# Attention's masks and first bias tables fetched during the projections, the gates reordered, and two pieces of the third branch done elsewhere

## The chip, the cores and the metric

One core of a Trainium2 chip runs the whole program. The metric is device time in microseconds (us) of one execution; a kernel's time is the median of its runs. A profile of one execution gives the start and length of every instruction on each engine: TensorE (PE, with its weight loads PEld), VectorE (DVE), ScalarE (ACT), GpSimd (POOL), SyncE (SP), and the DMA queues that SP, ACT and POOL issue on.

## The reference

Two layers of an encoder on 512 tokens of width 1024, in float32. Each layer is a half-step SwiGLU, a mixer, and a second half-step SwiGLU, each between RMS norms. The change lies in the mixer:

```python
u = pre(h); one combined projection of u ->
    A: 2-D neighbourhood attention on the 64-wide token grid (rel-pos bias), 8 heads
    B: sliding-window attention, 8 query heads on 2 key/value heads, rotary
    C: differential attention, 4 heads (two softmax maps, learned lambda, rotary)
    per-channel sigmoid gates (one per branch, 1024 channels each)
m = sum_i gate_i * (branch_i @ W_branch_i);  h = h + post(m @ W_out)
```

Branch A adds to its scores a bias table that depends on the head (`rpb`) and a mask for columns outside the window.

## The kernel before

All values are kept with channels on partitions: a 128x512 tile is 128 channels of the 512 tokens. A float32 product is made of three products of high and low parts (fp32r): `mm3` issues lines L326, L327 and L328 for each 128 input channels. Weights are streamed from DRAM as 512 KB tiles `wr` (L211, on SP's queue or ACT's), and split by ACT (L224, high part) and VectorE (L225, low part).

Each layer runs in phases: FFN 1 (`f`), `project` (`p`: most of the projection, by a seven-product scheme in groups; results that the mixer needs in another layout are stored to DRAM as `part` or `raw` by POOL, L1405), `mixer` (`m`: attention, gates, combination, output product), FFN 2 (`f`). Inside `project` and `mixer` a scheduler chooses each engine's order of instructions and the time at which a buffer is taken, from priorities that follow the order in which the code is written. On the chip every engine then works through its own list strictly in order; an instruction that waits holds up all that stands behind it on that engine, DMA issues on SP included.

The mixer's written order is the text `ORDER`, a list of units: `qa`p (load head pair p of branch A: bias tables `braw`, and the halves stacked as `st` tiles from `part`), `aa`p (its attention), `kb`, `qb`p, `ab`p (branch B), `qc`h, `ac`h, `fc`h (branch C: load with rotary, attention, final norm), `ga`/`gb`/`gc`m (gate m of a branch, 24 dense matmuls and a tanh) and `ya`/`yb`/`yc`m (combination m: 12 dense matmuls of the branch's output with `w_branch`, times the gate, added to the sum).

Names and lines that the change touches, in the kernel before:

- `mixer` L1702 to L1712: two tiles `mask` are loaded from `tables` (L1706), `ask` loads `braw` for one head (L1712). `biases` (the adds at L1723) makes a head's `bedge` and `bmid` from `braw` and `mask`, on VectorE. L1662 adds the bias to the scores and takes the row maximum (`nmx`).
- Loads: `load` (L1739), rotary `rope` (L1747 to L1750; VectorE's first operation on the loaded tile is L1748), `restacked` (L1762, L1763: the `st` tiles).
- Gates (L1898, ACT). Those of branch A stay in SBUF in two tiles of the pool `n`, [128, 4, 512] each; the others go to DRAM (L1901) and come back through `load` at their combination.
- `combine`: L1911 (VectorE) multiplies; for branches B and C, L1915 (POOL) adds to `merged[m]`. After that `M` splits `merged` (ACT L355, VectorE L356).
- Branch C's outputs `oc` are split (L352, L353) into tiles of pool `g`, which has 10 buffers; branch A's outputs `oa` are two tiles of pool `X` (6 buffers, four of which hold the operand until the last gate). The output norm's gains (`gain`, four loads on SP, L465) take a tile of pool `X`.
- The buffer that a loaded gate of branch B takes (pool `gd`, 2 buffers) is the one that a fresh gate takes on its way to DRAM.

Of the kernel before, what the change touches and what calls it, by code (L numbers as in the profile page):

```python
# [10 lines left out]
F32 = mybir.dt.float32  # L11
F32R = mybir.dt.float32r
AF = mybir.ActivationFunctionType
ALU = mybir.AluOpType
AX = mybir.AxisListType

P = 128
# [3 lines left out]
T = 512  # L21
# [18 lines left out]
QA, KA, VA, QB, KB, VB, QC, KC, VC, GL = 0, 4, 8, 12, 16, 17, 18, 22, 26, 30  # L40
COVER = (QA, KA, VA, QA + 1, KA + 1, VA + 1, KB, VB)
GROUPS = (
    (QA + 2, KA + 2), (VA + 2, VA + 3), (QA + 3, KA + 3), (QB, QB + 1), (QB + 2, QB + 3), (QC, KC), (QC + 1, KC + 1),
    (VC, VC + 1), (QC + 2, KC + 2), (QC + 3, KC + 3), (VC + 2, VC + 3),
) + tuple((GL + 2 * i, GL + 2 * i + 1) for i in range(0))
# [21 lines left out]
RPBW = 64  # L67
# [2 lines left out]


ORDER = """
qa0 qa1 aa0 ga0 ga1 qa2 aa1 ga2 qa3 aa2 ga3 ga4 kb qb0 aa3 ga5 qb1 ab0
ga6 ga7 gb0 qb2 ab1 gb1 gb2 qb3 ab2 ya0 gb3 ya1 gb4 qc0 ab3 ya2 gb5 ya3
qc1 ac0 gb6 ya4 gb7 qc2 fc0 ac1 ya5 gc0 ya6 fc1 qc3 ac2 gc1 ya7 gc2 fc2
ac3 yb0 gc3 yb1 gc4 fc3 yb2 gc5 yb3 gc6 yb4 gc7 yb5 yb6 yb7 yc0 yc1 yc2
yc3 yc4 yc5 yc6 yc7
"""


# [39 lines left out]
def encoder_kernel(ctx: ExitStack, tc: tile.TileContext, order, xT, wts, cols, rows, rpb, consts, tables, out):  # L120
    nc = tc.nc
# [3 lines left out]
    sb = ctx.enter_context(tc.tile_pool(name="sb", bufs=1))  # L125
# [4 lines left out]
    BUFS = {"X": 6, "n": 2, "wr": 3, "wp": 2, "wq": 2}  # L130
# [16 lines left out]
    def nm(s):  # L147
        serial[0] += 1
        return f"{s}{serial[0]}"

    def big(tag, dt=F32, shape=(P, T), name="v"):
        if tag in BUFS:
            return sb.tile(list(shape), dt, tag=tag, name=nm(name), bufs=BUFS[tag])
        kind, pool = phase[0]
        return pool.tile(list(shape), dt, tag=tag, name=nm(name), bufs=ABUFS[kind][tag])
# [7 lines left out]
    V, A, G, PE = nc.vector, nc.scalar, nc.gpsimd, nc.tensor  # L163

    def f(t):
        return t.bitcast(F32)
# [15 lines left out]
    def col(name, l, b=0, t=None):  # L182
        c = COLS[name, l] + b
        return (colt if t is None else t)[:, c : c + 1]
# [76 lines left out]
    for l in range(L):  # L261
        for which in (1, 2):
            name = f"ffn{which}_w_down"
# [81 lines left out]
    def dense1(name, l, c, X, r0=0, tag="mm", midway=None):  # L345
        return dense([(name, l, r0, c)], X, (tag,), midway=midway)[0]

    def split(src, tag="a", scale=None, shape=(P, T)):
        hi = big(tag, F32R, shape, name="hi")
        lo = big(tag, F32R, shape, name="lo")  # L350
        if scale is None:
            A.activation(hi, src, AF.Copy)  # L352
            V.tensor_tensor(out=lo, in0=src, in1=f(hi), op=ALU.subtract)  # L353
        else:
            A.activation(hi, src, AF.Copy, scale=scale)  # L355
            V.scalar_tensor_tensor(out=lo, in0=src, scalar=scale, in1=f(hi), op0=ALU.mult, op1=ALU.subtract)  # L356
        return hi, lo
# [1010 lines left out]
    def project(l, op, accs):  # L1368
        w, X = "w_in", op.blocks
# [76 lines left out]
        def work(n):  # L1446
            for _ in range(min(n, len(slowly))):
                slowly.pop(0)()
# [32 lines left out]
        made = {}  # L1481
# [38 lines left out]
        for n, c0 in (("cosR", 0), ("sinR", 512)):  # L1520
            t = big("rr", name=n)
# [22 lines left out]

        made["gates"] = []

        def gate_tile(c):
            if (c - GL) % 4 == 0:
                made["gates"].append(sb.tile([P, 4, T], F32, tag="n", name=nm("gate"), bufs=BUFS["n"]))
            return made["gates"][-1][:, (c - GL) % 4, :]  # L1550
# [5 lines left out]
        def second_half(g):  # L1556
            evict(groups[g]["t"], GROUPS[g][0], groups[g]["a"], 1)
            if GROUPS[g][0] < GL:
                ready(GROUPS[g][0], groups[g]["t"])

        def other(g):
            c, v = GROUPS[g][1], groups[g]["v"]
            if c >= GL:
                evict(gate_tile(c), c, v, None, -1.0)
                return
            x = v if form_of(c) == "-" else big("t", name="x")
            evict(x, c, v, None, -1.0)
            ready(c, x)

        for g in range(count):  # L1570
            more, last = g + 1 < count, g + 1 == count
            S.p1(g)
            if g:
                S.add22(g - 1)
            S.low24(g)
            if more:
                S.high1(g + 1)
            S.seed(g)
            if more:
# [12 lines left out]
            if more:  # L1592
                S.high12(g + 1)
            if g:
                other(g - 1)
            S.p6(g)
            if more:
                S.low13(g + 1)
            else:
                ensure(stream["made"] + 2)  # L1600
            S.copy2(g)
            S.p4(g)
            S.add21(g)
            if last:
                S.p5(g)
                S.add22(g)
            S.p2(g)
            first_half(g)
            if more:
                S.low12(g + 1)  # L1610
                S.sum4(g + 1)
                if g + 2 < count:
                    S.fetches(g + 2)
                else:
                    fetch(1, nc.sync)
                S.p5(g)
                S.high24(g + 1)
            work(3)
        S.p3(count - 1)
        second_half(count - 1)  # L1620
        other(count - 1)
        work(len(slowly))
        return made

    def stacks(x, both):
        hi, lo = split(x, "tx")
# [74 lines left out]
    def mixer(l, op, made):  # L1701
        w, X = "w_in", op.blocks  # L1702
        masks, raws, turning = {}, {}, []
        for c0, n in ((0, 512), (512, 256)):
            m = big("g", name="mask")
            nc.sync.dma_start(m[:, :n], tables[:, 1024 + c0 : 1024 + c0 + n])  # L1706
            for b in range(0, n, 256):
                masks[(c0 + b) // 256] = m[:, b : b + 256]

        def ask(hd):  # L1710
            raw = raws[hd] = big("g", name="braw")
            nc.sync.dma_start(raw, bass.AP(rpb.tensor, (l * 8 + hd) * 16 * RPBW, [[RPBW, 8], [1, 16], [1, 8 * RPBW]]))  # L1712

        def biases(hd):
            raw = raws.pop(hd)
# [59 lines left out]
        OT = {}  # L1775
# [51 lines left out]

            pending.append(done)

        oc, totc = [], []  # L1830

        def attn_c(sq, sk, v):
            vh, vl = v
# [50 lines left out]
            follow(rest)  # L1884

        gate, merged = {}, [None] * KD
        gate0 = made["gates"]
        while len(gate0) < 2:
            gate0.append(sb.tile([P, 4, T], F32, tag="n", name=nm("gate"), bufs=BUFS["n"]))
        for _, c in GROUPS:  # L1890
            for m in (c - 1 - GL, c - GL) if c > GL else ():
                gate[0, m] = gate0[m // 4][:, m % 4, :]

        def gates(n, *ms):
            for m in ms:
                pg = dense1(w, l, GL + n * KD + m, X)
                t = gate0[m // 4][:, m % 4, :] if n == 0 else big("gd", name="gate")
                A.activation(t, pg, AF.Tanh, scale=0.5, bias=col("b_gate", l, n * KD + m))  # L1898
                if n:
                    d = dr.tile([P, T], F32, tag="gate", name=nm("gate"), bufs=4 * KD)  # L1900
                    nc.sync.dma_start(d, t)  # L1901
                    t = d
                gate[n, m] = t

        def combine(n, key, *ms):
            for m in ms:
                py = dense1("w_branch", l, m, [OT[key, k] for k in range(4)], r0=n * 4)
                t = gate.pop((n, m))
                if n:
                    t = load(t, tag="gd" if n == 1 else "tx")  # L1910
                V.scalar_tensor_tensor(out=t, in0=t, scalar=1.0, in1=py, op0=ALU.add, op1=ALU.mult)  # L1911
                if n == 0:
                    merged[m] = t
                else:
                    G.tensor_tensor(out=merged[m], in0=merged[m], in1=t, op=ALU.add)  # L1915

        def qkv_b(c):
            return restacked(c, c == KB)
# [10 lines left out]
        def finish_c(hd):  # L1929
            A.activation(totc[hd], totc[hd], AF.Sqrt)  # L1930
            V.reciprocal(out=totc[hd], in_=totc[hd])
            rep = spread(totc[hd], NT)
            V.scalar_tensor_tensor(
                out=oc[hd], in0=oc[hd], scalar=gsub[:, l : l + 1], in1=rep, op0=ALU.mult, op1=ALU.mult
            )
            OT["c", hd] = split(oc[hd], "g")

        held = {}

# [103 lines left out]
    X = accs = None  # L2043
    for l in range(L):
        with open_phase("f"):
            X, accs = ffn(l, 1, X, accs)
        with open_phase("p"):
            made = project(l, X, accs)
        with open_phase("m"):
            X, accs = mixer(l, X, made)  # L2050
        with open_phase("f"):
            X, accs = ffn(l, 2, X, accs)
# [59 lines left out]
```

## Time and profile before

| | us |
|---|---|
| median of 3 runs | 2403.28 (2402.62 to 2405.92) |
| the profiled execution's own time | 2402.72 |
| its span | 2401.0 |
| mixer of layer 0, first to last score and combination | about 507 to 870 |
| mixer of layer 1 | about 1697 to 2058 |

The span is the time from the first instruction to the last. "Busy" on PE means that matmuls are in flight. A row of a timeline gives start, length, engine, line, operation and tiles, and in brackets the idle time in front of it and what ended that; a letter q behind an engine (SPq) is its instruction queue, where DMAs are issued. A list of waits gives, for each pair of waiting line and releaser, the us in total, the times and the longest.

### The profile page before, as it was taken

Reading aid. Unit: us, or ns where it says so; the run is one execution under the profiler, and the core shown is the slowest. Engines: PE = TensorE matmul, PEld = TensorE weight load, DVE = VectorE, ACT = ScalarE, POOL = GpSimd, SP = SyncE. Lnnn points to the kernel's source line nnn. Section 1 sums busy time; section 2 is a strip of 40 time slices with the busy share of each in tenths; the row PEclk is TensorE's granted clock in tenths of the full one; section 3 lists DMA queues with packets and bytes.
Section 4 is the critical chain, followed back from the end, with each engine's and each line's share of the span. In section 5 each row is a group of like instructions: output and inputs, shape, how many; then the busy total and the mean of one; then the engine's idle time right before and its main releaser. Section 6 shows DMA issues by size and latency. Waiting matters only on the chain. (4 is left out here: it accounts for less than half of the span.)

```text
span 2401.0 us, 39975 instructions
## 1 busy us (share of the span) xinstructions
PE 2350.9 (98%) x15062; PEld 2104.9 (88%) x15062; DVE 1874.5 (78%) x3040; ACT 1447.4 (60%) x2711; POOL 205.8 (9%) x258
## 2 busy tenths in 40 slices
PE   9999999999999999999999999999899999999998
PEld 8999889987877789998899998899788777899987
DVE  8887978957977567888878878888488765788796
ACT  6565666658766465555655555666586664656563
POOL 0111001110001300110001110011000012011100
PEclk9999999999999999999999999999999999999999
DMA  5566536667565434655435565366765664346642
GB/s 169 159 174 186 166 131 189 202 199 203 151 191 180 142 118 141 159 167 166 168 97 163 163 176 193 107 206 206 207 188 149 205 189 136 97 148 169 191 145 85
DMA packets 143265, 395.14 MB, mean 165 GB/s; under 512 B 19296, under 2 KB 26080, under 8 KB 142560
## 3 DMA queue, kind: packets, MB, share of 16 engines
q1 hardware_dynamic: 114672, 279.25, 37.5%
q0 software_dynamic: 12992, 57.68, 9.3%
q10 hardware_dynamic: 15408, 55.66, 7.7%
q8 instruction: 118, 1.93, 0.3%
q14 instruction: 75, 0.61, 0.1%
HBM read 326.98 MB, written 80.74 MB: 170 GB/s over the span
## 5 line engine op out<-in xcount | busy, mean ns | idle before, releaser
L680 PE MATMUL mm<-X,h 128*128 128x256 f32 x1472 | 261.5, 277 | 0.0
L225 DVE TENSOR_TENSOR w<-wr,w 128x512 fp32r<-128x512 f32 x272 | 189.2, 706 | 71.0 <-ACT w L224 70.2
L326 PE MATMUL mm<-X,w 128*128 128x512 f32 (+1 forms) x602 | 229.6, 381 | 3.0 <-ACT X L553 1.8
L327 PE MATMUL mm<-X,w 128*128 128x512 f32 (+1 forms) x602 | 229.9, 382 | 0.8 <-DVE X L554 0.7
L328 PE MATMUL mm<-X,w 128*128 128x512 f32 (+1 forms) x602 | 228.3, 379 | 1.7 <-DVE w L225 1.7
L224 ACT ACTIVATE w<-wr 128x512 fp32r<-128x512 f32 x272 | 167.5, 627 | 99.3 <-PE mm L328 54.2
L680 PEld LDWEIGHTS mm<-X,h 128*128 128x128 f32 x1472 | 223.5, 188 | 0.8 <-DVE v L738 0.2
L680 PE MATMUL mm<-ht,l 128*128 128x256 f32 x736 | 205.9, 280 | 0.0
L680 PE MATMUL mm<-ht,h 128*128 128x256 f32 x736 | 205.5, 279 | 0.0
L680 PE MATMUL mm<-lt,h 128*128 128x256 f32 x736 | 204.9, 278 | 0.0
L680 PE MATMUL mx<-ht,h 128*128 128x256 f32 x736 | 203.6, 277 | 0.1
L680 PE MATMUL mx<-lt,h 128*128 128x256 f32 x736 | 203.6, 277 | 0.0
L680 PE MATMUL mm<-X,l 128*128 128x256 f32 x736 | 203.5, 277 | 0.0
L680 PE MATMUL mx<-ht,l 128*128 128x256 f32 x736 | 203.5, 276 | 0.0
L630 DVE TENSOR_TENSOR l<-wr,h 128x1024 fp32r<-128x1024 f32 x92 | 112.5, 1223 | 61.0 <-PE mm L680 60.9
L662 ACT ACTIVATE h<-wr 128x1024 fp32r<-128x1024 f32 x92 | 97.7, 1062 | 72.4 <-PE mx L680 52.7
L680 PE MATMUL at<-X,w 128*128 128x256 f32 x1104 | 141.2, 277 | 0.0
L680 PEld LDWEIGHTS mm<-ht,l 128*128 128x128 f32 x736 | 138.7, 188 | 0.1
L680 PEld LDWEIGHTS mm<-lt,h 128*128 128x128 f32 x736 | 138.7, 188 | 0.0
L680 PEld LDWEIGHTS mm<-ht,h 128*128 128x128 f32 x736 | 138.6, 188 | 0.0
L680 PEld LDWEIGHTS mx<-ht,h 128*128 128x128 f32 x736 | 138.2, 188 | 0.3 <-ACT v L724 0.3
L680 PEld LDWEIGHTS mx<-lt,h 128*128 128x128 f32 x736 | 138.3, 188 | 0.0
(438 smaller groups left out, 6770.7 us busy)
## 6 DMA issues: line engine op xcount, KB each, us to landing
wr<-in_wts_dram SPq DMA_DIRECT2D x269, 512.0 KB
wr<-in_wts_dram ACTq DMA_DIRECT2D x106, 512.0 KB
sum<-in_wts_dram POOLq DMA_DIRECT2D x64, 512.0 KB, 5.0
st<-part SPq DMA_DIRECT2D x120, 128.0 KB
ap<-in_wts_dram SPq DMA_DIRECT2D x20, 512.0 KB
a<-kept SPq DMA_DIRECT2D x32, 256.0 KB
ap<-sum SPq DMA_DIRECT2D x16, 512.0 KB
x<-part SPq DMA_DIRECT2D x32, 256.0 KB
```

The costliest lines, as they stand in the source:

```text
L224: A.activation(hi, raw, AF.Copy)
L225: V.tensor_tensor(out=lo, in0=raw, in1=f(hi), op=ALU.subtract)
L326: PE.matmul(acc, w[0], x[0], start=start, stop=False)
L327: PE.matmul(acc, w[0], x[1], start=False, stop=False)
L328: PE.matmul(acc, w[1], x[0], start=False, stop=stop)
L630: V.tensor_tensor(out=w["l1"], in0=self.raws[g][0], in1=f(w["h1"]), op=ALU.subtract)
L662: A.activation(self.W[g]["h24"], self.raws[g][1], AF.Copy)
L680: PE.matmul(acc, ws[i], xs[j], start=start and k == m == 0, stop=stop and k == n - 1 and m == 2, skip_group_check=True,)
```

## The change

Four things are changed together.

1. `project` gets `tables_of_a`, called in the written order at group 6 of its loop. It takes one tile `pre` of pool `n` and loads both masks and the bias tables of heads 0 and 1 into it; `mixer` uses these parts where it used `mask` and the first two `braw`. The second of branch A's gate tiles can only be taken when `pre` has been read for the last time.
2. `ORDER`: gates gb0 to gb7 stand ahead of ga4 to ga7, and the combinations of branch A come later. All combinations of branch A still precede those of B and C.
3. Branch C's heads 1 to 3 are split into two tiles of pool `X` (`pairs`) instead of tiles of pool `g`. Head 0 stays in `g`.
4. The sum of branch C's part is made on VectorE instead of POOL; branch B's stays on POOL.

```diff
@@ -70,11 +70,11 @@
 ORDER = """
-qa0 qa1 aa0 ga0 ga1 qa2 aa1 ga2 qa3 aa2 ga3 ga4 kb qb0 aa3 ga5 qb1 ab0
...
+qa0 qa1 aa0 ga0 ga1 qa2 aa1 ga2 qa3 aa2 ga3 gb0 kb qb0 aa3 gb1 qb1 ab0
...
@@ -1544,6 +1544,14 @@
+        def tables_of_a():
+            t = sb.tile([P, 4, T], F32, tag="n", name=nm("pre"), bufs=BUFS["n"])
+            nc.sync.dma_start(t[:, 0, :], tables[:, 1024 : 1024 + 512])
+            nc.sync.dma_start(t[:, 1, :256], tables[:, 1024 + 512 : 1024 + 768])
+            for hd in range(2):
+                nc.sync.dma_start(t[:, 2 + hd, :], raw_of(l, hd))
+            made["tables"] = t
+
@@ -1616,11 +1624,16 @@
             work(3)
+            if g == 6:
+                tables_of_a()
...
+    def raw_of(l, hd):
+        return bass.AP(rpb.tensor, (l * 8 + hd) * 16 * RPBW, [[RPBW, 8], [1, 16], [1, 8 * RPBW]])
@@ -1701,15 +1714,16 @@
-        for c0, n in ((0, 512), (512, 256)):
-            m = big("g", name="mask")
-            nc.sync.dma_start(m[:, :n], tables[:, 1024 + c0 : 1024 + c0 + n])
-            for b in range(0, n, 256):
-                masks[(c0 + b) // 256] = m[:, b : b + 256]
+        pre = made["tables"]
+        for n in range(3):
+            masks[n] = pre[:, n // 2, 256 * (n % 2) : 256 * (n % 2) + 256]
 
         def ask(hd):
+            if hd < 2:
+                raws[hd] = pre[:, 2 + hd, :]
+                return
             raw = raws[hd] = big("g", name="braw")
...
@@ -1884,16 +1898,13 @@
-        gate0 = made["gates"]
-        while len(gate0) < 2:
-            gate0.append(sb.tile([P, 4, T], F32, tag="n", name=nm("gate"), bufs=BUFS["n"]))
...
+        gate0 = []
 
         def gates(n, *ms):
             for m in ms:
                 pg = dense1(w, l, GL + n * KD + m, X)
+                if n == 0 and m % 4 == 0:
+                    gate0.append(sb.tile([P, 4, T], F32, tag="n", name=nm("gate"), bufs=BUFS["n"]))
@@ -1912,7 +1923,7 @@
-                    G.tensor_tensor(out=merged[m], in0=merged[m], in1=t, op=ALU.add)
+                    (G if n == 1 else V).tensor_tensor(out=merged[m], in0=merged[m], in1=t, op=ALU.add)
@@ -1933,7 +1944,14 @@
-            OT["c", hd] = split(oc[hd], "g")
+            if hd == 0:
+                OT["c", hd] = split(oc[hd], "g")
+                return
+            if not pairs:
+                pairs.extend(sb.tile([P, 4, T], F32R, tag="X", name=nm("oc"), bufs=BUFS["X"]) for _ in range(2))
+            hi, lo = OT["c", hd] = tuple(t[:, hd, :] for t in pairs)
+            A.activation(hi, oc[hd], AF.Copy)
+            V.tensor_tensor(out=lo, in0=oc[hd], in1=f(hi), op=ALU.subtract)
```

The new `ORDER` as a whole:

```
qa0 qa1 aa0 ga0 ga1 qa2 aa1 ga2 qa3 aa2 ga3 gb0 kb qb0 aa3 gb1 qb1 ab0
gb2 gb3 qb2 ab1 gb4 gb5 gb6 qb3 ab2 gb7 ga4 qc0 ab3 ga5 ga6 qc1 ac0
ga7 ya0 gc0 ya1 qc2 fc0 ac1 gc1 ya2 gc2 ya3 gc3 fc1 qc3 ac2 ya4 ya5
ya6 ya7 yb0 gc4 fc2 ac3 yb1 gc5 yb2 gc6 fc3 yb3 gc7 yb4 yb5 yb6 yb7
yc0 yc1 yc2 yc3 yc4 yc5 yc6 yc7
```

In the changed kernel the lines below the new function are 11 to 14 higher: the bias adds of L1723 stand at L1737, L1662 at L1675, the `st` loads at L1776 and L1777, `braw` at L1726, L1739 at L1753, L1911 at L1922 and L1915 at L1926.

The rows that follow are the order of instructions on one engine (line, operation, written tile and read tiles with buffer numbers), as the two programs have it in layer 0. First SyncE, where the mixer starts; before:

```order
L1706 DMA mask_5789<-in_tables_dram 128x512
L1706 DMA mask_5791<-in_tables_dram 128x256
L1712 DMA braw_5797<-in_rpb_dram 128x1x512
L1712 DMA braw_5799<-in_rpb_dram 128x1x512
L1712 DMA braw_5801<-in_rpb_dram 128x1x512
L1712 DMA braw_5803<-in_rpb_dram 128x1x512
L1762 DMA st_5805<-part_4051 64x512
L1763 DMA st_5805<-part_4053 64x512
```

And with the change, at the same place:

```order
L1726 DMA braw_5796<-in_rpb_dram 128x1x512
L1726 DMA braw_5798<-in_rpb_dram 128x1x512
L1776 DMA st_5800<-part_4051 64x512
L1777 DMA st_5800<-part_4053 64x512
L1776 DMA st_5803<-part_4051 64x512
```

Masks and the tables of the first two heads are gone from here (the two `braw` left are the second pair's). The second `braw` waits for the project's last stores, as a mask did before. The four loads that left stand here on SyncE now, in the middle of the project:

```order
L1549 DMA pre_5225<-in_tables_dram 128x512
L1550 DMA pre_5225<-in_tables_dram 128x256
L1552 DMA pre_5225<-in_rpb_dram 128x1x512 x2
L211 DMA wr_4271<-in_wts_dram 128x1024
L1454 DMA sh_4202<-x_4200 32x512 x4
```

`wr_4271` is the weight tile that was issued at 386.06 us in the profile of before; the four loads were moved to just ahead of it.

Second, VectorE where the mixer starts, around the first bias; before, with the splits of three weight tiles ahead of it:

```order
L1411 TENSOR_TENSOR lo_5777<-at_5771,hi_5776 128x512
L225 TENSOR_TENSOR w_5973<-wr_5971,w_5973 128x512
L225 TENSOR_TENSOR w_5988<-wr_5971,w_5988 128x512
L225 TENSOR_TENSOR w_6184<-wr_6182,w_6184 128x512
L1723 TENSOR_TENSOR bedge_5828<-braw_5797,mask_5789 128x256
L1723 TENSOR_TENSOR bmid_5829<-braw_5797,mask_5789 128x256
```

With the change:

```order
L1411 TENSOR_TENSOR lo_5782<-at_5776,hi_5781 128x512
L225 TENSOR_TENSOR w_5969<-wr_5967,w_5969 128x512
L1737 TENSOR_TENSOR bedge_5823<-pre_5225 128x256
L1737 TENSOR_TENSOR bmid_5824<-pre_5225 128x256
L1737 TENSOR_TENSOR bedge_5823<-pre_5225 128x128 x2
```

Two splits now come after the first bias. Its wait is no longer for `braw` but for the last two `part` stores of POOL's queue.

Third, the tail. SyncE, with the change (gates of branch B, written `x_9038` and so on, are loaded for yb4 to yb7):

```order
L460 DMA h_9305<-kept_3724 128x512 x2
L460 DMA h_9305<-kept_3805 128x512 x2
L465 DMA gain_9314<-in_rows_dram 128x512 x4
L1753 DMA x_9038<-gate_7096 128x512
L1912 DMA gate_9018<-gate_9016 128x512
L1753 DMA x_9058<-gate_7133 128x512
L1753 DMA x_9080<-gate_7170 128x512
L1753 DMA x_9100<-gate_7366 128x512
```

The gains stood some 35 rows earlier before, around a rotary load of branch C: their tile now takes a buffer of the operand, which the gate gc7 reads last. VectorE in the last combinations (yc2 and yc3), with the change:

```order
L1922 SCALAR_TENSOR_TENSOR x_9164<-x_9164,mm_9146 128x512
L225 TENSOR_TENSOR w_9191<-wr_9189,w_9191 128x512
L1926 TENSOR_TENSOR gate_5964<-gate_5964,x_9164 128x512
L1922 SCALAR_TENSOR_TENSOR x_9184<-x_9184,mm_9168 128x512
L356 SCALAR_TENSOR_TENSOR lo_9281<-gate_5964,hi_9280 128x512
L1926 TENSOR_TENSOR gate_5964<-gate_5964,x_9184 128x512
L225 TENSOR_TENSOR w_9211<-wr_9189,w_9211 128x512
```

The two L1926 of these rows were POOL's before, as L1915.

More of the change, by code (lines that the diff above doesn't have):

```diff
@@ L72 @@
 ORDER = """
-qa0 qa1 aa0 ga0 ga1 qa2 aa1 ga2 qa3 aa2 ga3 ga4 kb qb0 aa3 ga5 qb1 ab0
[L74 to L77, printed above, removed]
+qa0 qa1 aa0 ga0 ga1 qa2 aa1 ga2 qa3 aa2 ga3 gb0 kb qb0 aa3 gb1 qb1 ab0
[3 more added lines that the diff above has]
+yc0 yc1 yc2 yc3 yc4 yc5 yc6 yc7
 """
@@ L1703, in mixer @@
         masks, raws, turning = {}, {}, []
-        for c0, n in ((0, 512), (512, 256)):
-            m = big("g", name="mask")
-            nc.sync.dma_start(m[:, :n], tables[:, 1024 + c0 : 1024 + c0 + n])
-            for b in range(0, n, 256):
-                masks[(c0 + b) // 256] = m[:, b : b + 256]
+        pre = made["tables"]
+        for n in range(3):
+            masks[n] = pre[:, n // 2, 256 * (n % 2) : 256 * (n % 2) + 256]
         def ask(hd):
+            if hd < 2:
+                raws[hd] = pre[:, 2 + hd, :]
+                return
             raw = raws[hd] = big("g", name="braw")
-            nc.sync.dma_start(raw, bass.AP(rpb.tensor, (l * 8 + hd) * 16 * RPBW, [[RPBW, 8], [1, 16], [1, 8 * RPBW]]))
+            nc.sync.dma_start(raw, raw_of(l, hd))
         def biases(hd):
@@ L1828, in attn_b @@
             pending.append(done)
-        oc, totc = [], []
+        oc, totc, pairs = [], [], []
         def attn_c(sq, sk, v):
@@ L1886, in mixer @@
         gate, merged = {}, [None] * KD
-        gate0 = made["gates"]
-        while len(gate0) < 2:
-            gate0.append(sb.tile([P, 4, T], F32, tag="n", name=nm("gate"), bufs=BUFS["n"]))
-        for _, c in GROUPS:
-            for m in (c - 1 - GL, c - GL) if c > GL else ():
-                gate[0, m] = gate0[m // 4][:, m % 4, :]
+        gate0 = []
         def gates(n, *ms):
```

## The prediction

> **What bounds the kernel.** I read the page's first part first, then TensorE's waits stage by stage, then the stretches in which those waits fall.
>
> ```profile
> span 2401.0 us, 39975 instructions
> PE 2350.9 (98%) x15062; PEld 2104.9 (88%) x15062; DVE 1874.5 (78%) x3040; ACT 1447.4 (60%) x2711; POOL 205.8 (9%) x258
> ```
>
> TensorE (PE) is busy for all but 50.1 us, and the change leaves its matmuls as they are: what it can win is a part of these 50 us. They are shared out by the four lists below, of TensorE's waits in both layers' mixers: 505 to 560 us (start, layer 0), 560 to 880 (the rest of it), 1695 to 1740 (start, layer 1) and 1740 to 2062 (the rest). Columns: waiting line, releaser, us in total, times, longest.
>
> ```profile
> PE mx L1659 <- DVE nmx L1662: 4.5, 2, 2.3
> PE mx L1659 <- DVE l L1676: 3.0, 1, 3.0
> ...
> PE mm L326 <- DVE x L1911: 3.9, 5, 1.3
> PE o L1870 <- DVE lo L353: 2.0, 1, 2.0
> PE o L1694 <- DVE lo L353: 1.1, 1, 1.1
> ...
> PE mx L1659 <- DMA st<-part: 6.0, 2, 3.5
> PE mx L1659 <- DVE nmx L1662: 2.1, 2, 1.7
> ...
> PE mm L326 <- DVE x L1911: 4.5, 5, 1.7
> PE o L1870 <- DVE lo L353: 1.5, 1, 1.5
> PE o L1694 <- DVE lo L353: 1.5, 1, 1.5
> ```
>
> Three groups: the **start** of branch A (7.5 + 8.1 = 15.6 us), the **middle** (2.0 + 1.1 + 1.5 + 1.5 = 6.1), and the gate combination L1911, nearly all of it at the **tail** (3.9 + 4.5 = 8.4). Together 30.1 us, 1.25% of the span: the most that any rearrangement of the mixer could give back.
>
> **Start: masks and first biases.** Layer 0, in order of time (start, length, engine, line):
>
> ```profile
> 509.76 0.54 POOL L1405 DMA_DIRECT2D part<-lo  x1
> ...
> 514.31 0.33 SPq L1706 DMA_DIRECT2D mask<-in_tables_dram  x1
> 514.83 2.90 SPq L1712 DMA_DIRECT2D braw<-in_rpb_dram  x4
> 517.82 0.53 SPq L1762 DMA_DIRECT2D st<-part  x1
> ...
> 520.08 0.43 DVE L1723 TENSOR_TENSOR bedge<-braw,mask 128x256 f32<-128x256 f32 x1 [2.75 <-DMA braw<-in_rpb_dram]
> ...
> 524.46 0.42 DVE L1723 TENSOR_TENSOR bedge<-braw,mask 128x256 f32<-128x256 f32 x1 [2.54 <-DMA braw<-in_rpb_dram]
> ...
> 507.58 0.40 PE L326 MATMUL mm<-X,w 128*128 128x512 f32 x1
> ...
> 518.49 0.39 PE L326 MATMUL mm<-X,w 128*128 128x512 f32 x1
> ...
> 521.64 0.51 PE L1659 MATMUL mx<-early 128*128 128x256 f32 x2 [2.31 <-DVE nmx L1662]
> ```
>
> SyncE's queue issues in order. The mask waits there for the project's last stores to land, so the four bias loads go out from 514.83 and the first can be added only at 520.08; the score that needs it runs 1.56 us later, at 521.64. The second head pays the same again at 524.46.
>
> With the change both heads' tables are in SBUF long before. The order on VectorE shows that the first L1737 waits instead for the project's last two stores. Their landing:
>
> ```profile
> part<-hi POOLq DMA_DIRECT2D x2, 256.0 KB, 5.0
> part<-lo POOLq DMA_DIRECT2D x2, 256.0 KB, 4.9
> ```
>
> The last is issued at 509.76 and lands 4.9 to 5.0 us on, at 514.7. The put starts there, and with the same 1.56 us TensorE can go on at about 516.3. The program now has 38 dense matmuls instead of 51 ahead of that score; the first and the 49th of them above are 10.91 us apart, 0.227 a matmul, so that 38 last from 507.58 to 516.2. The wait of 2.31 becomes about 0.2, and the second head's goes entirely: nmx in both layers falls from 4.5 + 2.1 to 0.4. Bounds: 0, and the whole 6.6 if the stores land as much later as the loads did.
>
> The other 9.0 us of the start are stacked operands (`st`). SyncE's own waits, layer 0, then layer 1:
>
> ```profile
> SPq L1763 <- DMA wr<-in_wts_dram: 6.0, 1, 6.0
> ...
> SPq L1763 <- DMA wr<-in_wts_dram: 8.0, 2, 4.8
> ```
>
> The 3.0 that the list puts on `l` in layer 0 is the second operand half, held up by the `wr` in the first row: `l` was long done. In the new order two bias loads instead of two masks and four bias loads stand ahead of the `st` loads, which begin about 515.4 instead of 517.82; and the second head pair's `st` no longer wait behind a weight load of ACT's queue. Against that, TensorE asks for its first `st` 12 dense matmuls (2.7 us) and 4.3 us of removed waits sooner. I keep 1.0 us in layer 0 and 2.5 in layer 1 (the size of the wait in layer 1 that no `wr` explains), 3.5 of the 9.0; bounds 0 and 9.0. The start's sum: 15.6 − 0.4 − 3.5 = **11.7 us saved**.
>
> **The fetch itself.** Masks and two heads are 0.9 MB a layer, on SyncE's queue just ahead of the weights that are issued at 386.06. The stretch has:
>
> ```profile
> 380.00:390.00 10.00, 10.00 (x48) 8.26 (x47) 6.81 (x10) 5.85 (x11) 2.16 (x4) 1.00 0.78 247
> ...
> 386.06 0.33 SPq L211 DMA_DIRECT2D wr<-in_wts_dram  x1
> ...
> 393.86 1.04 ACT L625 ACTIVATE h<-wr 128x1024 fp32r<-128x1024 f32 x1
> ```
>
> (The row gives us, PE, PEld, DVE, ACT, POOL busy with counts, clock, DMA share, GB/s.) At 247 GB/s the extra bytes are 3.6 us of transfer; the weights of 386.06 are read 7.8 us later with no wait, and PE is busy for all 10 us. I take 0.5 us a layer, bounds 0 and 3.6.
>
> The Trainium skill, "DMA: Bandwidth & Descriptors", section "Issuing engines are not separate DMA queues", speaks against any such move: transfers from the SyncE, ScalarE and GpSimd queues run on the same 16 engines and interleave, so an early fetch is paid for by whatever else is moving. By it the project's weights and stores would slow by the whole transfer, and the sum would be 6.2 us worse; the trace agrees that a busy stretch stretches transfers, but shows no wait of PE there.
>
> **Tail.** Third part's sums, layer 1:
>
> ```profile
> 2001.00 1.61 POOL L1915 TENSOR_TENSOR gate<-gate,x 128x512 f32<-128x512 f32 x1 [2.13 <-DVE x L1911]
> 2004.74 1.61 POOL L1915 TENSOR_TENSOR gate<-gate,x 128x512 f32<-128x512 f32 x1 [2.13 <-DVE x L1911]
> ...
> 2002.64 0.63 ACT L355 ACTIVATE hi<-gate 128x512 fp32r<-128x512 f32 x1 [2.59 <-POOL gate L1915]
> ...
> 2003.30 0.69 DVE L356 SCALAR_TENSOR_TENSOR lo<-gate,hi 128x512 fp32r<-128x512 f32 x1 [1.85 <-ACT hi L355]
> 2003.91 0.68 DVE L1911 SCALAR_TENSOR_TENSOR x<-x,mm 128x512 f32<-128x512 f32 x1
> ```
>
> It is a loop: add on POOL, high part on ACT, low part L356, then the next L1911 behind it on VectorE, which frees the PSUM bank PE waits for, then POOL again: 3.74 us a turn. PE's 12 matmuls a unit take 12 x 0.227 = 2.73 us, so it waits. On VectorE the add costs what L1911 costs, 0.68: the turn is 3.74 − 1.61 + 0.68 = 2.8, and in half of the pairs L1922 stands ahead of the low part. These waits go. The 8 adds a layer are 5.4 us of VectorE, paid out of its idle 1.85 us a turn.
>
> What stays is the second part's loads:
>
> ```profile
> 1980.31 1.68 POOL L1915 TENSOR_TENSOR gate<-gate,x 128x512 f32<-128x512 f32 x1 [7.41 <-DVE x L1911]
> ...
> 1982.01 12.99 SPq L1739 DMA_DIRECT2D x<-gate  x4
> ...
> 1985.75 0.69 DVE L1911 SCALAR_TENSOR_TENSOR x<-x,mm 128x512 f32<-128x512 f32 x1 [1.72 <-DMA x<-gate]
> ...
> 1986.59 0.47 PE L326 MATMUL mm<-hi,w 128*128 128x512 f32 x1 [1.65 <-DVE x L1911]
> ...
> 1924.21 0.50 PE L326 MATMUL mm<-hi,w 128*128 128x512 f32 x1 [0.95 <-DVE x L1911]
> ```
>
> A load waits for the POOL sum that frees its buffer and takes 1985.75 − 1982.01 = 3.74 us. The new order runs yb4 to yb7 without a gate between them. With 2.73 a unit on PE and 3.74 + 0.69 + 1.68 for a buffer, counted by hand from the end of yb3 (yb4 done at 5.45 + 2.73 = 8.2 with gc7 between): yb5's load is issued at 8.2 + 0.69 + 1.68 = 10.5 and used at 14.2, where PE wanted its bank at 13.7 (about 1.2 wait with L1922 itself); yb7's costs another 0.5 at yc1. So 1.7 us a layer, and the 0.95 of the last row, which lies before the tail, stays. 8.4 becomes 4.4: **4.0 saved**. Bounds: 8.4 saved, or the rival on the slower side below.
>
> The post-norm gains, which used to be loaded early, now wait for gc7 on SyncE and stand ahead of yb4's load:
>
> ```profile
> L465 SPq DMA_DIRECT2D gain<-in_rows_dram x8: 333/422/900, 712.2 to 1904.8; - x8
> ```
>
> Four issues of 0.42 after the middle of gc7 put yb4's load 4.4 us after yb3, landed at 8.1, needed at 8.2: just covered by gc7 and yb4 on PE.
>
> **Middle.** These waits come from VectorE standing in L1748 (branch C's rotary multiply) for its load, with the low part that PE needs behind it; the row, from the list of that line, gives the idle time in us and the times. The change does not touch that; between the first and last attention of branch C ORDER now has 8 gates and 9 combinations where it had 6 and 6, so more cover. I take 0; bounds: all 6.1 gone, or 7.9 lost (all 14.0 us that L1748 waits reaching PE).
>
> ```profile
>   DMA x<-raw: 14.0, 7
> ```
>
> **Sum**, against the profiled execution's own 2402.72 us (0.56 below the median of the runs, 2403.28): 2402.72 − 11.7 − 4.0 + 1.0 = **2388.0 us**.
>
> **Rivals.** (1) *The stores replace the loads.* VectorE, now holding the first put in order, waits for the stores, and `st` stays as late as now: the two second-head waits (4.5 − 2.3 and 2.1 − 1.7, from the nmx rows, so 2.6) and the tail remain as gains: 2402.72 − 2.6 − 4.0 + 1.0 = 2397.1. For it: every `st` still stands behind a store-bound load on SyncE. Against: that load is one, not six. (2) *The fetch is paid in the project*: the weights of 386.06 come later by its whole transfer and PE stands for it, 3.6 instead of 0.5 a layer, so 2388.0 + 6.2 = 2394.2. Against: no wait there now. (It is the case that the section of the Trainium skill named above would have one expect.) (3) *Slower: the tail becomes bound by its loads.* Each us by which yb5's and yb7's loads exceed 3.74 comes back about twice, since they follow one another through the same two buffers. The gains are broadcast loads in one burst with `h` right ahead of them, and a burst of bias loads took 520.08 − 514.83 = 5.3 and more, up to 9 for the second. At 9.5 us a load, a layer's tail costs 1.7 + 2 x 5.8 = 13.3 and the time is 2402.72 − 11.7 − 7.4 + 1.0 + 2 x 13.3 = 2411.2; it is slower than before from some 7.4 us a load. Against: the loads of the rows above took half of that. (4) *The change does not do what it says*: the fetch stays late because its tile is not free early. The order puts it directly ahead of the weights of 386.06 with nothing left to wait for, so this is unlikely: 2402.72 − 4.0 = 2398.7, the tail alone.
>
> **Chances.** Forecast 0.62 (own range 2381 to 2396); stores 0.18; fetch 0.07; slower tail 0.08; not as said 0.05. Range 2380 to 2402: it leaves out the slow tail and a middle that vanishes too. A run here can tell about 0.2%, 4.8 us: faster 0.78 (the forecast, the fetch, half of the stores' case), same 0.13, slower 0.09.
>
> **What would show it.** Right: L1737's first row at about 515, nmx waits under 1 us, the gate L1922 waits after yc1 gone, turns of 2.7 us on VectorE, the rope idle as now. Wrong: SyncE's first `st` after 517; weights waiting around 380 to 400; x<-gate over 5 us at the tail, with L1922 idle for DMA; or new waits of low parts L353 behind a put.

## The result and the profile after

| | before | after |
|---|---|---|
| median of 4 runs, us | 2403.45 (2402.62 to 2405.92) | 2382.69 (2380.20 to 2386.78) |
| the profiled execution's own time | 2402.72 | 2380.20 |
| its span | 2401.0 | 2378.4 |

The ratio of the times is 0.9914 (95%: 0.9896 to 0.9931): the kernel became 20.8 us faster; 15.3 had been forecast. The two profiled executions are 22.5 us apart, and the readings below explain that difference.

First the page of the changed kernel, its busy times:

```profile
PE 2346.9 (99%) x15062; PEld 2105.4 (89%) x15062; DVE 1883.2 (79%) x3056; ACT 1448.5 (61%) x2711; POOL 178.8 (8%) x242
```

TensorE's idle time went from 50.1 to 31.5 us (span less busy), which is 18.6 of the 22.6 us of span. Its *busy* time fell too, by 4.0 us, with the same 15062 matmuls: keep that in mind for the end of this section.

TensorE's waits in the changed kernel's mixers, in four lists as before: start and rest of layer 0, start and rest of layer 1 (505 to 560 us, 560 to 880, 1680 to 1725, 1725 to 2050):

```profile
PE at L1703 <- ACT s L1692: 1.5, 1, 1.5
...
PE mm L326 <- DVE x L1922: 2.2, 1, 2.2
PE o L1707 <- DVE lo L353: 1.9, 2, 1.5
...
PE at L1880 <- DVE s L1871: 0.7, 1, 0.7
...
PE o L1706 <- ACT hi L352: 0.3, 1, 0.3
...
PE at L1703 <- ACT s L1692: 1.3, 1, 1.3
...
PE mm L326 <- DVE x L1922: 2.7, 2, 2.3
PE at L1880 <- DVE s L1871: 1.3, 1, 1.3
PE o L1707 <- DVE lo L353: 1.2, 3, 0.7
...
PE mx L1672 <- DMA st<-part: 0.7, 1, 0.7
...
PE o L1706 <- ACT hi L352: 0.3, 1, 0.3
```

Start: 1.5 + 1.3 + 0.7 = 3.5 us, where it was 15.6. Combination: 2.2 + 2.7 = 4.9, where it was 8.4. The rest: 5.7, where the four lists of before add up to 8.7 once their start, L1911 and the final norm's unchanged waits (L553, L554) are taken out. Together 14.1 against 32.7.

The start of layer 0 in the changed kernel, in order of time:

```profile
514.31 0.66 SPq L1726 DMA_DIRECT2D braw<-in_rpb_dram  x1
...
514.90 0.43 DVE L1737 TENSOR_TENSOR bedge<-pre 128x256 f32<-128x256 f32 x1 [2.35 <-DMA part<-lo]
515.07 0.51 SPq L1776 DMA_DIRECT2D st<-part  x1
```

The first bias is added at 514.90 instead of 520.08, and what releases it is the project's last store (`part<-lo`), not a bias load. The first `st` load goes out at 515.07 instead of 517.82.

What busy time gained is seen in the windows. Columns: stretch, its length, busy time and count of PE, PEld, DVE, ACT, POOL, then the granted clock of TensorE, DMA share and GB/s. Before:

```profile
505.00:560.00 55.00, 47.30 (x242) 39.35 (x242) 27.18 (x90) 33.35 (x88) 2.14 (x4) 0.91 0.71 188
...
524.11:530.94 6.83, 5.65 (x18) 4.77 (x19) 4.16 (x18) 4.90 (x16) 0.00 (x0) 0.50 0.67 182
548.00:551.42 3.42, 2.89 (x9) 2.43 (x10) 0.05 (x1) 0.00 (x0) 0.00 (x0) 0.50 0.68 197
722.08:725.49 3.41, 3.41 (x11) 2.85 (x11) 3.10 (x6) 1.23 (x2) 0.00 (x0) 0.50 0.47 154
1735.84:1739.25 3.41, 2.80 (x9) 2.34 (x10) 0.00 (x0) 0.00 (x0) 0.00 (x0) 0.50 0.78 232
```

After:

```profile
505.00:560.00 55.00, 53.39 (x301) 44.79 (x301) 37.88 (x127) 42.92 (x119) 2.14 (x4) 1.00 0.79 218
...
784.86:788.27 3.41, 3.19 (x8) 2.55 (x9) 1.59 (x3) 0.00 (x0) 2.96 (x2) 0.50 0.48 154
1962.46:1965.87 3.41, 3.28 (x8) 2.63 (x9) 1.29 (x2) 0.00 (x0) 2.94 (x2) 0.50 0.45 156
```

Compare the first rows: the same 55 us hold 301 matmul records instead of 242, but only 6 us more of busy time. Before, matmuls there ran at a mean clock of 0.91. The other rows are all the stretches of the two kernels' mixers in which the granted clock was 0.50. Half of the busy time in them is given away: (5.65 + 2.89 + 3.41 + 2.80) x 0.5 = 7.4 us before, (3.19 + 3.28) x 0.5 = 3.2 after. So by this estimate some 4.1 us of the gain are not waits at all, but the slow matmuls that followed them. The prediction has no such term.

### The profile page after: what moved, and what is told of

Same layout as the page of the kernel before. It is cut to its first block, busy times and chain, and to the rows that moved or that the text cites. A ratio compares the mean times of both kernels' runs of the same rounds, so it can differ in the third digit from the quotient of the medians.

```text
span 2378.4 us, 39981 instructions
## 1 busy us (share of the span) xinstructions
PE 2346.9 (99%) x15062; PEld 2105.4 (89%) x15062; DVE 1883.2 (79%) x3056; ACT 1448.5 (61%) x2711; POOL 178.8 (8%) x242
## 5 line engine op out<-in xcount | busy, mean ns | idle before, releaser
L326 PE MATMUL mm<-X,w 128*128 128x512 f32 (+1 forms) x602 | 228.5, 380 | 2.0 <-ACT X L553 1.8
```

The costliest lines, as they stand in the source:

```text
L326: PE.matmul(acc, w[0], x[0], start=start, stop=False)
```

## The experiments

Times are medians; each kernel is set against runs of the kernel before on the same chip. "The fetch" is part 1 of the change, "the order" part 2, "the pairs" part 3, "the sum" part 4.

| kernel | us | before, us | difference | ratio (95%) |
|---|---|---|---|---|
| sum alone | 2399.67 | 2404.04 | −4.4 | 0.9985 (0.9976 to 0.9993) |
| fetch alone | 2394.84 | 2403.65 | −8.8 | 0.9965 (0.9953 to 0.9977) |
| fetch + sum | 2390.99 | 2402.58 | −11.6 | 0.9951 (0.9940 to 0.9963) |
| fetch + order | 2386.25 | 2402.58 | −16.3 | 0.9928 (0.9915 to 0.9941) |
| fetch + order + sum (no pairs) | 2381.05 | 2404.04 | −23.0 | 0.9907 (0.9894 to 0.9921) |
| whole change | 2382.69 | 2403.45 | −20.8 | 0.9914 (0.9896 to 0.9931) |
| fetch + order + pairs (no sum) | 2391.39 | 2404.04 | −12.7 | 0.9948 (0.9936 to 0.9961) |
| order + pairs + sum (no fetch) | 2405.94 | 2404.04 | +1.9 | 1.0009 (0.9999 to 1.0020) |
| whole change, late gate loads elsewhere | 2376.14 | 2403.65 | −27.5 | 0.9883 (0.9864 to 0.9901) |
| the same without the pairs | 2373.94 | 2403.65 | −29.7 | 0.9876 (0.9862 to 0.9891) |

### The sum alone

```diff
-                    G.tensor_tensor(out=merged[m], in0=merged[m], in1=t, op=ALU.add)
+                    (G if n == 1 else V).tensor_tensor(out=merged[m], in0=merged[m], in1=t, op=ALU.add)
```

> The kernel before with one thing changed: branch C's sum on VectorE. If the loop POOL, ACT, VectorE is what held yc2 to yc7 (the prediction), the L1911 waits of 0.7 us or so at the tail (three in each layer) go and the time falls by 4 to 5 us, to about 2399. If those waits only stand in for the loads of the gates, it stays at 2403.

Measured 4.4 us faster. The list of TensorE's waits has `PE mm L326 <- DVE x L1911: 5.6, 4, 1.9`, where before had 8.4 us in 10 waits: six short waits are gone and four stay. Ahead of two of them, 1.9 us each, VectorE waits for a gate's load; the other two (0.6 and 1.2) lie before the tail.

### The sum back on POOL

The line above undone in the changed kernel.

> The changed kernel with branch C's sum back on POOL. By the loop: waits of about 0.7 us come back at each yc from yc2 on, 4 to 6 us in both layers, so about 2387. If the order or the gates' loads set the tail: no change, 2383.

Measured 8.7 us slower than the changed kernel, more than expected. Ten waits on L1922 are 10.2 us, among them the six that the sum alone had removed: 5.3 more than in the changed kernel, of the 12.0 us between the two profiled executions (2392.18 and 2380.20). Waits for `st` loads and low parts of attention are longer in it as well. The sum is worth 4.4 alone, 2.8 on top of the fetch (11.6 − 8.8), and 6.7 on top of fetch and order (23.0 − 16.3). By the intervals of the table each such difference of two rows is uncertain by some 4 us, so these three can't be told apart.

### Everything but the fetch

```diff
-            if g == 6:
-                tables_of_a()
...
-        pre = made["tables"]
-        for n in range(3):
-            masks[n] = pre[:, n // 2, 256 * (n % 2) : 256 * (n % 2) + 256]
+        for c0, n in ((0, 512), (512, 256)):
+            m = big("g", name="mask")
+            nc.sync.dma_start(m[:, :n], tables[:, 1024 + c0 : 1024 + c0 + n])
...
-            if hd < 2:
-                raws[hd] = pre[:, 2 + hd, :]
-                return
```

> The changed kernel with masks and bias tables loaded at the mixer's start again, all else kept (new ORDER, branch C's tiles, sum on VectorE). If the early fetch makes the gain (the prediction, and the TensorE clock that falls to half after the waits it removes), the nmx and st waits of the start return and the time rises by 11 to 16 us, to 2394 to 2399. If the new order of gates makes it (the rival), the time stays within 3 us of 2383.

The whole gain went: 1.9 us slower than before, and 23.3 slower than the changed kernel, twice what the start holds. Its waits over the whole span (its lines are 2 or 3 lower than in the changed kernel):

```profile
PE mx L1670 <- DVE nmx L1673: 5.6, 3, 3.6
PE mx L1854 <- ACT e L1861: 5.1, 4, 1.6
PE at L1877 <- DVE s L1868: 4.3, 4, 1.7
...
PE mx L1670 <- DMA st<-part: 3.3, 2, 3.1
...
PE mx L1670 <- DVE l L1687: 2.7, 1, 2.7
```

The start's waits are back (5.6 + 3.3 + 2.7), as the theory has it. But 9.4 us on L1854 and L1877, branch C's scores and the transposes of its attention weights, are in neither of the two kernels to this size. The profiled execution, 2398.45, is the fastest of this kernel's eleven, so its waits stand for 18 us of the 23.3 at most. The parts don't add up, and the next experiments ask why.

### The fetch alone

Part 1 in the kernel before, with a small change of `ORDER` that the gate tiles ask for: ga4 to ga7 come one gate later, gb0 in front of them.

```diff
-qa0 qa1 aa0 ga0 ga1 qa2 aa1 ga2 qa3 aa2 ga3 ga4 kb qb0 aa3 ga5 qb1 ab0
-ga6 ga7 gb0 qb2 ab1 gb1 gb2 qb3 ab2 ya0 gb3 ya1 gb4 qc0 ab3 ya2 gb5 ya3
+qa0 qa1 aa0 ga0 ga1 qa2 aa1 ga2 qa3 aa2 ga3 gb0 kb qb0 aa3 ga4 qb1 ab0
+ga5 ga6 ga7 qb2 ab1 gb1 gb2 qb3 ab2 ya0 gb3 ya1 gb4 qc0 ab3 ya2 gb5 ya3
...
+            if g == 6:
+                tables_of_a()
```

> The kernel before with the early fetch alone; ORDER is that of before but for ga4 to ga7 and gb0, which trade places so that gate a's second tile is taken after the tables are read. If the fetch makes the gain: the waits of the start fall from 15.6 to some 4 us and TensorE's clock stays full behind them, so the time falls by 12 to 18 us, to 2386 to 2392. If it needs the other parts to come out (waits that move into the middle of the mixer), 2396 or more.

8.8 us faster, between the two cases of the expectation. The start did what it should (1.3 + 1.2 in layer 0, 1.2 + 0.2 in layer 1, no `nmx` at all). The rest of the mixers gave part of it back; its waits over the span:

```profile
PE o L1884 <- DVE lo L353: 3.8, 2, 2.2
PE o L1707 <- DVE lo L353: 3.8, 4, 2.3
...
PE at L1880 <- DVE nm L1860: 2.8, 2, 1.4
```

L1884 (L1870 before) is the output product of branch C's attention, L1707 that of the others. With L1706 (1.1 us for VectorE's L1710) that is 11.5 us in the middle, where before had 6.1 on low parts. So the early start was won, and 5 us of it came back as waits of branch B and C. Here the step "middle: 0" of the prediction breaks.

### The fetch with the new order, and with the sum

These two tell whether it is the order or VectorE's sum that keeps the middle quiet.

> The early fetch and the new ORDER, without the other two parts (branch C in pool g, all sums on POOL). With the old order the fetch alone left 11.5 us of waits in the attention of branches B and C (L1707, L1884, L1880, L1706). If the new ORDER is what removes those, they fall to 5 or less, the three yc waits in each layer stay, and the time is 2385 to 2390. If ORDER does nothing by itself, it is e3_fetch_alone's 2395.

> The early fetch in the old order (as e3_fetch_alone) with branch C's sum on VectorE. If fetch and sum are independent, it is e3_fetch_alone's 2395 less e1_sum_alone's gain of 4.4: 2390 to 2391, with the middle's waits as they are there. If the sum's 5 us on VectorE collide with the rest of its work, 2393 or more; if they together give what the whole change gives, 2383.

With the order 16.3 us, with the sum 11.6: the order adds 7.5 to the fetch's 8.8, the sum 2.8. What the order does is seen at L1762 (L1748 before), the rotary multiply behind which the low parts stand in VectorE's queue. The list of that line gives the idle time of VectorE ahead of it and the times. Fetch alone, the old order:

```profile
  DMA x<-raw: 10.9, 6
  DMA sh<-raw: 1.0, 1
```

Fetch and sum, the old order:

```profile
  DMA x<-raw: 8.3, 5
  DMA sh<-raw: 4.6, 2
```

Fetch and new order:

```profile
  DMA x<-raw: 3.5, 2
```

The changed kernel:

```profile
  DMA x<-raw: 3.7, 2
```

The kernel without the fetch, but with the order (L1759 there):

```profile
  DMA x<-raw: 19.2, 11
  DMA sh<-raw: 2.1, 1
```

With the old order VectorE stands 12 to 14 us for the rotary loads, with or without fetch and sum; with fetch and new order 3.5. With the new order and no fetch it stands 21.3, more than ever. The order is thus worth 7.5 us behind the fetch (16.3 − 8.8), and without it nothing: order, pairs and sum together are +1.9, where the sum alone was −4.4. Why these loads come late in the one case and not in the other, I did not follow through SyncE's queue. That the stall goes when the order is new and the fetch is early is what the rows show; that it sets the size of the middle's waits they do not: the kernel before has 14.0 us of stall with 6.1 of such waits, the fetch alone 11.9 with 11.5.

### Without the pairs

```diff
-            if hd == 0:
-                OT["c", hd] = split(oc[hd], "g")
-                return
-            if not pairs:
-                pairs.extend(sb.tile([P, 4, T], F32R, tag="X", name=nm("oc"), bufs=BUFS["X"]) for _ in range(2))
-            hi, lo = OT["c", hd] = tuple(t[:, hd, :] for t in pairs)
-            A.activation(hi, oc[hd], AF.Copy)
-            V.tensor_tensor(out=lo, in0=oc[hd], in1=f(hi), op=ALU.subtract)
+            OT["c", hd] = split(oc[hd], "g")
```

> The changed kernel with branch C's heads 1 to 3 split into the pool g again, so that the gains can be loaded early and the operand tiles are left alone. If the tiles of pool g were the hindrance (splits of oc waiting for combinations of branch B), the time rises by 1 to 4 us with waits ahead of yc; if they cost nothing, it stays at 2383, or falls by up to 2 us since gains no longer stand ahead of yb4's load.

2381.05 us: the same as the whole change, or a little better. The pairs bring nothing here. What they cost is in the changed kernel's tail (layer 1, in order of time; x4 are the four gain loads):

```profile
1947.49 1.92 SPq L465 DMA_DIRECT2D gain<-in_rows_dram  x4
1949.51 0.44 SPq L1753 DMA_DIRECT2D x<-gate  x1
...
1956.51 0.69 DVE L1922 SCALAR_TENSOR_TENSOR x<-x,mm 128x512 f32<-128x512 f32 x1 [3.21 <-DMA x<-gate]
1961.76 0.69 DVE L1922 SCALAR_TENSOR_TENSOR x<-x,mm 128x512 f32<-128x512 f32 x1 [2.25 <-DMA x<-gate]
...
1957.26 0.50 PE L326 MATMUL mm<-hi,w 128*128 128x512 f32 x1 [0.41 <-DVE x L1922]
...
1962.59 0.77 PE L326 MATMUL mm<-hi,w 128*128 128x512 f32 x1 [2.32 <-DVE x L1922]
```

The pairs take buffers of pool `X`, so the gains wait for them and go out right in front of yb4's load. That load, issued at 1949.51, is used at 1956.51: 7.0 us, not 3.74 (in layer 0 it is 4.8, from 774.20 to 779.04). TensorE loses 0.41 and then 2.32. Without the pairs the same waits are 0.6 us in each layer.

### The late gate loads in another pool

If the tail's rest is a load that can't start before its buffer is free, then other buffers should remove it, pairs or not.

```diff
-                    t = load(t, tag="gd" if n == 1 else "tx")
+                    t = load(t, tag="tx" if n == 2 else "st" if m > 3 else "gd")
```

> The changed kernel with the gates of yb4 to yb7 loaded into four tiles of the pool st, which is idle at that time, instead of the two of gd. If the tail's last waits are those loads behind POOL's sums, as the prediction has it, the L1922 waits of 2.2 and 2.3 us go, and with them the half clock that follows each: 5 to 8 us less, 2375 to 2378. If other things end the tail's waits, 2381 to 2383.

6.5 us faster than the changed kernel; the two ratios' intervals overlap by a little. No wait on L1922 is left in the list of TensorE's waits.

Both edits together:

> The same with branch C's heads 1 to 3 in pool g, as in e5_no_pairs: both tail waits were small there already (0.6 each). If tile pool X for branch C is of no use, 2378 to 2381; if the st loads help only beside it, 2383 or more.

2373.94 us, faster than expected and the fastest of all: 29.7 us below the kernel before, where the change gained 20.8; here the intervals are apart. The place of the last listing, in this kernel's windows:

```profile
1955.00:1970.00 15.00, 15.00 (x67) 12.32 (x66) 12.76 (x19) 6.29 (x11) 5.18 (x3) 1.00 0.41 122
```

PE is busy for all of the 15 us at full clock, where the changed kernel waited 2.7 us (0.41 + 2.32) and gave away 1.6 more at half clock (half of the 3.28 in the row of 1962.46). In neither mixer of this execution does the clock fall at all.

### Made gaps: when does the clock drop?

The changed kernel with made waits in the output product: a transpose, a chain of VectorE operations on its result, and a transpose of that.

```diff
+        def gap(n):
+            b = bank("mx")
+            PE.transpose(b[:, :P], ident, ident)
+            V.tensor_copy(out=junk, in_=b[:, :P])
+            for _ in range(n - 1):
+                V.tensor_tensor(out=wide, in0=wide, in1=wide, op=ALU.mult)
+            V.tensor_tensor(out=junk, in0=junk, in1=wide[:, :P], op=ALU.mult)
+            PE.transpose(b[:, :P], junk, ident)
```

> The changed kernel with made waits of TensorE, in the output product where its order is fixed: a transpose waits for a chain of VectorE operations. Lengths by the 0.69 us of such an operation: about 2.0 and 3.4 us alone in layer 0; 2.7 alone and 2.0 twice, 1.4 us apart, in layer 1. If a wait costs only itself, the granted clock stays 1.00 behind all of them and the run is 12 us longer in all. If TensorE's clock falls after waits of over 2 us, as the profile of before suggests, windows at 0.5 follow the longer ones and the pair, each costing 1.3 to 2.8 us more than the wait.

One run, 2396.73 us. The five second transposes, with the wait ahead of each in brackets:

```profile
819.86 0.33 PE L2012 MATMUL mx<-cons,junk 128*128 128x128 f32 x1 [2.04 <-DVE junk L2011]
...
846.05 0.33 PE L2012 MATMUL mx<-cons,junk 128*128 128x128 f32 x1 [3.49 <-DVE junk L2011]
...
2004.61 0.33 PE L2012 MATMUL mx<-cons,junk 128*128 128x128 f32 x1 [2.76 <-DVE junk L2011]
...
2029.35 0.33 PE L2012 MATMUL mx<-cons,junk 128*128 128x128 f32 x1 [2.04 <-DVE junk L2011]
...
2033.22 0.33 PE L2012 MATMUL mx<-cons,junk 128*128 128x128 f32 x1 [2.04 <-DVE junk L2011]
```

And this kernel's windows around and behind them, columns as above. They are cut where the granted clock can change: in the traces here it falls and rises at the ends of intervals of 3.413 us (the last section shows it).

```profile
815.83:819.24 3.41, 1.99 (x10) 1.31 (x8) 1.98 (x5) 0.63 (x1) 0.00 (x0) 1.00 0.23 90
819.24:822.65 3.41, 2.79 (x13) 2.30 (x14) 1.13 (x3) 0.00 (x0) 0.00 (x0) 1.00 0.33 72
...
843.14:846.55 3.41, 0.50 (x3) 0.47 (x4) 3.27 (x7) 2.19 (x5) 0.00 (x0) 1.00 0.00 0
846.55:849.96 3.41, 3.41 (x10) 2.63 (x9) 2.41 (x7) 1.84 (x6) 0.00 (x0) 0.50 0.49 97
...
2000.26:2003.67 3.41, 1.59 (x8) 1.00 (x6) 1.94 (x5) 0.63 (x1) 0.00 (x0) 1.00 0.18 71
2003.67:2007.08 3.41, 2.47 (x11) 2.06 (x12) 1.45 (x3) 0.00 (x0) 0.00 (x0) 1.00 0.27 62
...
2027.57:2030.98 3.41, 1.63 (x8) 1.25 (x8) 1.66 (x4) 2.52 (x5) 0.00 (x0) 1.00 0.00 0
2030.98:2034.39 3.41, 1.38 (x8) 1.00 (x7) 3.10 (x7) 0.00 (x0) 0.00 (x0) 1.00 0.00 0
2034.39:2037.80 3.41, 3.41 (x10) 2.64 (x9) 2.38 (x6) 2.20 (x6) 0.00 (x0) 0.50 0.60 202
```

Behind 2.04 us alone and 2.76 alone the clock stays at 1.00. Behind 3.49, and behind the second 2.04 of the pair, it is 0.50 for 3.41 us, which gives away 3.41 x 0.5 = 1.7 us beyond the wait itself. The intervals tell these cases apart, by TensorE's idle time in one of them (length less busy). The single 2.04 lies across a boundary, 1.42 + 0.62 us, and so does the 2.76, 1.82 + 0.94. The 3.49 leaves 2.91 in one interval. Of the pair, the first leaves 1.78 in its interval and the clock stays; the second lies wholly in the next one, 2.03, and the clock falls. So it is not the nearness of two waits that counts here, nor the length alone, but how much of an interval stands idle.

## Why the prediction was right, and where it was not

**Start: right, in place and size.** 15.6 fell to 3.5 us, 12.1 saved where 11.7 stood. `nmx` fell to nothing (0.4 was left to it), the first L1737 came at 514.90 (about 515), held by the project's stores, and `st` kept 0.7 of its 9.0 us. What remains besides is of another kind (L1703, the attention weights, 2.8) and was not forecast: the prediction left 3.5 us to `st`, and that 0.7 + 2.8 comes to the same 3.5 is luck. Rival (1), that the stores take the loads' place, has the releaser right and the rest wrong: VectorE does wait for them, but TensorE does not, and the first `st` load goes out 2.75 us earlier (515.07 against 517.82).

**The fetch: right, within what can be told.** The first score stands at 507.69 instead of 507.02 and in layer 1 the stretch up to it is 0.7 us longer too: 1.4 us where 1.0 was taken; rival (2) asked 7.2. But the executions scatter by as much: that score stands at 507.02 to 507.27 in the traces of the three kernels without the fetch and at 506.73 to 508.62 in the nine with it. So the 7.2 is excluded, and the 1.4 is no finer than that. (What the Trainium skill states in "DMA: Bandwidth & Descriptors", "Issuing engines are not separate DMA queues", that all these queues share the same 16 engines, did not decide here: the prediction had reckoned from it that the project could pay the whole transfer.)

**Tail: 3.5 saved where 4.0 stood, by a partly different way.** Six waits of the yc loop went, as reckoned: the sum put back brings them back, and alone it gives 4.4 us. But the step "just covered by gc7 and yb4 on PE" failed. yb4's load took 7.0 us behind the burst of gains, and its wait and the next one's are 2.7 of the 4.9 us that stay. It is the burst that rival (3) names, but not the loads that it prices: yb5's load took 2.8 us (issued at 1958.99, used at 1961.76), less than 3.74, and what came late was yb4's alone. Taking the burst away (no pairs) leaves waits of 0.6 us in each layer, and taking other buffers (loads in `st`) removes them all. That the saving came to 3.5 beside a forecast of 4.0 is thus in part luck.

**Middle: "I take 0" was wrong in both directions.** The reason given was that the change does not touch the rotary loads' wait, and the forecast sign was "the rope idle as now". It fell from 14.0 to 3.7 us. The fetch alone would have brought the middle's waits from 6.1 to 11.5, and the new order more than removed that: all waits outside start and combination are 3.0 us less. The cause is the order of the units together with the fetch (the same order without the fetch stalls 21.3 us), not the cover by gates in front of VectorE's stall: what went is the stall.

**A term that was missing: the granted clock.** Some 4.1 us. The prediction priced each wait at its length. In the kernel before, the two waits at the first scores (2.31 us before 521.64, 2.19 before 525.29) have 0.94 and 1.01 us in the interval from 520.70 to 524.11, and from 524.11 on the clock is 0.50: 18 matmuls in 6.83 us, 2.6 a us, where the changed kernel has 301 in 55, 5.5 a us. This could be read from the trace of the kernel before, and was not looked for.

**The sum.** In the profiled executions: start −12.1, combination −3.5, other waits −3.0, fetch +1.4, clock −4.1: −21.3 of the −22.5 that they differ by; 1.2 us is unplaced. Forecast were −11.7, −4.0, 0, +1.0 and nothing. The terms that were priced carry the forecast; the profiled execution lies 7.8 us below it (2388.0 − 2380.20), and 7.1 of these are the two that were not, middle and clock. The median lies 5.3 below.

**What stays open.** The parts interact, and their single worths depend on what else is there; the 9.4 us of waits in branch C that the kernel without the fetch showed are not explained, nor is its wide spread (2398.45 to 2413.29). The pairs were slower in each of three comparisons (2382.69 against 2381.05; 2391.39 against 2386.25, on different chips; 2376.14 against 2373.94), but in no single one are the intervals clearly apart. Why the first `st` waits differ between kernels with the same start was not tried. The made gaps were run once.

## What to carry to other kernels

A wait of an engine that bounds the kernel is priced at its length only while the granted clock behind it stays at 1.00: look at the windows after each wait of some 2 us. Here some of these cost 1.7 us more and some nothing. An early load that starts a stage sooner is worth what the stage's later loads allow; without a new order some 5 of the 12 us won at the start were lost again further on. And a tile moved to another pool moves whatever waits for that pool: here four gain loads, to the one place where a load had no slack.

## What the runs showed of the hardware

TensorE's granted clock is either 1.00 or 0.50 in these traces, and it changes on a grid of time. In the kernel before it falls at 524.11, 548.00, 722.08 and 1735.84 us; the last three come 23.89, 197.97 and 1211.73 us after the first, which are 7, 58 and 355 steps of 3.413 us. There it stays down for one step (3.41 us) or two (6.83, from 524.11). In the changed kernel the falls at 784.86 and 1962.46 are 345 steps apart, in the one with made gaps those at 846.55, 1969.54 and 2034.39 are 329 and 19 steps apart.

What comes before a fall is an interval of that grid in which TensorE stood idle for about half of it or more. The twelve traces have 8192 intervals at full clock between 30 us from the start and 20 us from the end. All 19 with 1.9 us or more of idle time were followed by 0.50, 5 of the 27 with 1.5 to 1.9, and none of the others. So the edge lies between 1.5 and 1.9 us of 3.413; these traces don't place it closer.

A wait of some 2.3 us can therefore go either way, as it falls on a boundary or not. The kernel with made gaps has yb5's wait on L1922 in both layers: 2.39 us before 786.95 lies across the boundary at 785.11 and left the clock at 1.00; 2.26 before 1969.38 lies in the interval from 1966.12 to 1969.54, and the clock was 0.50 behind it. With the sum back on POOL it is the same: 2.35 us before 789.04 left it at 1.00, 2.33 before 1971.42 brought 0.50.

The Trainium skill, "TensorE: Matmul & The Clock Gate", section "HAM oscillation — how this bites in real kernels", gives the abstract rule that no idle gap should be over about 3.4 us; the 3.49 agrees, and the 2.04, 2.26 and 2.33 that brought 0.50 show that shorter gaps are not safe. The same page of the Trainium skill, in "What's actually happening", calls the window in which activity is judged free-running, so that equal waits could fall on either side. The traces agree: equal waits did.
